# Moving the operands of the large products to multiples of 512 bytes in SBUF

## The chip, the cores and the metric

The kernel runs on one core of one Trainium2 chip. The metric is the device time of one execution in microseconds (us). A core has a matrix engine (TensorE; PE in the profile, and PEld for its loads of stationary operands), a vector engine (VectorE, DVE), an activation engine (ScalarE, ACT), GpSimd (POOL) and a queue engine (SyncE, SP) that here only issues transfers. Working memory (SBUF) has 128 partitions; a tile lies at the same byte offset in every partition. Products are summed in PSUM.

A matrix product of the engine has a stationary operand, which is loaded first (128 rows of 128 columns here), and a moving operand, which streams through it column by column. Both are read from SBUF.

## The reference

One inference step of a four-layer network over 128 context tokens and 512 latent tokens of width 1024, in float32. Each layer has a token mixer and an MLP, each with modulation and a layer norm:

```
for l in range(4):                            # mixers: linear attention, conformer, short conv, linear attention
    h = x * (1 + scale) + shift               # modulation from the conditioning vectors
    x = layer_norm(alpha * x + gate * mixer(h))
    h = x * (1 + scale2) + shift2
    x = layer_norm(alpha * x + gate2 * (square(relu(h @ w1)) @ w2))    # w1 [1024, 4096], w2 [4096, 1024]
```

The mixers are themselves mostly products with weights [1024, 1024] to [1024, 3072]. Outputs are both token streams and the final states of the linear attention.

## The kernel before, in words

All 640 tokens are handled together, in five tiles of 128 tokens. Each large product is made of three products in a single-pass float32 format (float32r): weights and activations are split into a high and a low part, and high x high, high x low and low x high are summed in PSUM. The tiles in which these operands lie are:

- `hT` (L459): the sublayer's input, features on partitions, [128, 2 parts, 8 k tiles, 640 tokens]. `put_hT` (L394 to L399) and, for the first sublayer, `opening` (L530, L531) fill it.
- `whi`, `wlo` (L105, L106): the two parts of a weight tile [128, 1024], six buffers each. `split` makes them from the staged float32 tile `st` (L112, five buffers): ScalarE rounds (L107), VectorE subtracts (L108).
- `act` (L1160): the squared ReLU of the MLP, eight tiles [128, 2 parts, 640 tokens]; `a` (L1095): the same for the short convolution.

There are two kinds of large product. `mm1_steps` (L138 to L148) gives output with features on partitions: the weight part is stationary and `hT` moves, 384 tokens in one group and 256 in the next; a group is 8 k tiles x 3 = 24 matmuls. `mm2_steps` (L181 to L195) gives output with tokens on partitions: an activation tile (`hT`, `act` or `a`) is stationary and 512 columns of the weight part move; again 24 matmuls a group. Only the very last token tile of the kernel is done in two groups of 256 columns (`finish`, L916). Two smaller products in the same format form the gates of the linear attention (L685): the stationary operand is `low` or `za`, the moving one lies in the same `low` tile or in `wgb`. TensorE's order is written out by hand: a virtual clock (`beat`, L93) counts columns / 2400 us per matmul and puts work that waits for others between products.

SBUF tiles are placed by pools, one behind the other in the order in which pools and tiles are first asked for: `const` (`cm`, `ones`, `mhalf`, `hT`, `x0` to `x4`, `ident`, `prm`, `tri`, `mask`), then `stage` (`st`), `wp` (`whi`, `wlo`) and the others, and at the end a pool for the current sublayer. A tile's start is rounded up to 32 bytes. So a tile's size sets where everything behind it starts. `mhalf` (the constant -0.5, 8 columns), `ident` (a 128 x 128 identity), `cu0` and `cu1` (inputs of the short convolution) and `acc` (running sums of a modulation in the MLP) are such tiles. The starts, as the built program has them, in bytes within a partition:

| tile | start before | over a multiple of 512 |
|---|---|---|
| hT | 17696 | 288 |
| st | 84000 and each 4096 on | 32 |
| whi, wlo | 104480 to 149536, each 4096 on | 32 |
| za, wgb (gate products, heads 2 and 3) | 161824, 165920 | 32, 32 |
| low (gate products, heads 0 and 1) | 183360 and 198720 | 64 |
| a | 184384 and each 5120 on | 64 |
| act | 187392 and each 5120 on | 0 |

Within these tiles the slices that a matmul reads are whole multiples of 512 bytes apart (128 columns of 4 bytes, or 2560 or 20480 bytes), so the last column holds for each operand of the large products. The exception is the gates' first factor, whose weight tile has slices of 96 columns.

Of the kernel before, what the change touches and what calls it, by code (L numbers as in the profile page):

```python
# [38 lines left out]
class Filler:  # L39
    """Products for the tensor engine to run while a chain of dependent steps waits for other engines."""  # L40

# [25 lines left out]
class Net:  # L67
# [19 lines left out]

# [1 line left out]
    def after(self, us, fn):  # L89
# [12 lines left out]

# [1 line left out]
    def split(self, src, n=1024):  # L104
# [14 lines left out]
    @contextmanager  # L119
    def behind(self, t):  # L120
        """Keeps the vector engine's work in it behind the parts of token tile t's next input."""
        with ExitStack() as held:
            for half in range(2 if (t, 0) in self.marks else 0):
                held.enter_context(self.tc.issue_after(self.marks[t, half]))
            yield
# [10 lines left out]

# [1 line left out]
    def mm1_steps(self, ps, w, c0, n, m=128):  # L138
        """Yields the microseconds of each instruction, as the other generators of products do."""
        i = 0  # L140
        for kt in range(KT):
            for a, h in ((0, 0), (0, 1), (1, 0)):
                self.nc.tensor.matmul(  # L143
                    ps[:m, :n], w[a][:, kt * m:(kt + 1) * m], self.hT[:, h, kt, c0:c0 + n],
                    start=(i == 0), stop=(i == 3 * KT - 1),
                )
                i += 1
                yield self.beat(n / 2400)  # L148
# [24 lines left out]

# [1 line left out]
    def mm2(self, srcs, lhs, epi):  # L175
# [31 lines left out]

# [1 line left out]
    def mod_queue(self, l):  # L209
        """Queues layer l's modulation by groups of 2048 columns: a k tile at a time on the tensor engine, or,  # L210
        where the groups fall in an MLP, two k tiles of 512 columns at a time on the vector engine."""
        self.mods[l] = {"T": self.modp.tile([128, 48, 2], F32, tag="modT", name="modT", bufs=3)}
        for g in range(1 if l == self.layers[0] else 0, 3):
            if (l, g) in MOD_DVE:
                for v in (2 * g, 2 * g + 1):
                    for half in range(2):
                        for p in range(4):
                            self.fill.append((l, g, partial(self.mod_dve, l, v, half, p)))
            else:
                for kt in range(KT):  # L220
                    self.fill.append((l, g, partial(self.mod_step, l, g, kt)))
# [21 lines left out]
    def tail(self, us, fn):  # L243
        """Runs fn once: us later, or before the next part of a modulation."""
        def once():
            if self.mod_tail is once:
                self.mod_tail = None
                fn()

        self.mod_tail = once  # L250
        self.after(us, once)

    def mod_bank(self, l, cols):
        """A bank for the sums, and the bias of each quarter of its rows."""
        ps = self.ps.tile([128, 512], F32, tag="md", name="md", bufs=1)
        mrow = self.row.tile([128, 512], F32, tag="mrow", name="mrow")
        n = 128 // len(cols)
        for t, c in enumerate(cols):
            self.nc.gpsimd.dma_start(
                mrow[n * t:n * t + n, :], self.d["mod_b"][l:l + 1, c:c + 512].broadcast_to([n, 512]))  # L260
        return ps, mrow
# [39 lines left out]
    def mod_dve(self, l, v, half, p):  # L301
        """Vector v's half: two k tiles more of the products, added up per partition; the tensor engine sums those."""
        nc, m = self.nc, self.mods[l]
# [44 lines left out]
    def affine(self, l, sub, prev):  # L348
        """A, B with modulate(LN(x)) = xhat * A + B per feature; prev = (l, i) of the LN."""
        nc = self.nc  # L350
# [23 lines left out]

# [1 line left out]
    def stats(self, a, b, eps):  # L376
        """mean, (var + eps) ** -0.5 and -mean * that over two [128, 512] halves."""
        nc = self.nc
# [15 lines left out]
    def put_hT(self, hf, k0, t):  # L394
        """hf [128, n, 128]: features of k tiles k0.. of token tile t, split into hT."""
        dst = lambda h: self.hT[:, h, k0:k0 + hf.shape[1], t * 128:(t + 1) * 128]
        self.nc.scalar.copy(dst(0), hf)
        self.mark = self.nc.vector.tensor_tensor(out=dst(1), in0=hf, in1=dst(0).bitcast(F32), op=AL.subtract)  # L398
        self.marks[t, k0 > 0] = self.mark.ins  # L399
# [47 lines left out]

# [1 line left out]
    def start(self):  # L449
# [6 lines left out]
        nc.vector.memset(self.ones, 1.0)  # L456
        self.mhalf = const.tile([128, 8], F32, name="mhalf")
        nc.vector.memset(self.mhalf, -0.5)
        self.hT = const.tile([128, 2, KT, NTOK], F32R, name="hT")  # L459
        self.x = [const.tile([128, D], F32, name=f"x{t}") for t in range(TT)]  # L460
        self.mod_queue(self.layers[0])
        self.constant("ident", [128, 128])
        self.units = []
# [13 lines left out]
    def opening(self, products, raw, tmp):  # L477
        """The first sublayer's input, k tile by k tile as its shift and scale come in: unit u of the first
        layer's modulation holds those of features 128 u.. for all inputs. products(u): what tile u is for."""
        nc = self.nc  # L480
# [57 lines left out]

# [1 line left out]
    def gla(self, l, j, nxt):  # L540
        nc, d, tc = self.nc, self.d, self.tc
        with ExitStack() as ctx:
# [8 lines left out]
            def gate_w(dst, hd):  # L551
                """Two heads of the gates' second factor, against z_hi, z_lo, z_hi and 1, 1: w_hi, w_hi, w_lo, b_hi, b_lo."""
                st = self.stage.tile([128, 1024], F32, tag="st", name="st")
# [112 lines left out]
            def chunks(a, par):  # L666
                """[128, 640] -> the chunks of one parity: [128, 5, 64]."""
                return a.rearrange("p (c b k) -> p c b k", b=2, k=64)[:, :, par]
# [4 lines left out]
            def core1(hd):  # L673
# [34 lines left out]
                for i in range(2):  # L708
# [3 lines left out]
                    self.mark = nc.vector.tensor_tensor(out=Em[i], in0=q[hd, 1], in1=Em[i], op=AL.mult)  # L712
                # per tile: the keys of the chunk that comes first, decayed to its end, and both chunks' decay
                F1 = q[hd, 0].rearrange("p (d c k) -> p d c k", d=2, k=64)
# [171 lines left out]
    def out_proj(self, w, lhs, nxt, last):  # L886
        """The sublayer's last product with the residual, and the layer norm token tile by token tile."""
        self.mm2(w[0], lhs, self.residual(0))
# [11 lines left out]
    def finish(self, w, lhs):  # L900
        """The last token tile, its second half of columns in two parts to have less to do after the last product."""
        nc, t = self.nc, TT - 1
# [31 lines left out]

# [1 line left out]
    def conformer(self, l, j, nxt):  # L936
        nc, d, tc = self.nc, self.d, self.tc
        with ExitStack() as ctx:
# [50 lines left out]
            def convolve(c, scr, meanwhile=None):  # L989
                """Four taps of 32 channels a pass: partition (s, channel) holds the row shifted by s."""  # L990
                f = 5 * ROW
# [21 lines left out]
            def add_bias():  # L1013
                """x += b_pw2 * gate, for the second product's bias."""
                self.flush()
# [68 lines left out]

# [1 line left out]
    def shortconv(self, l, j, nxt):  # L1086
        nc, d, tc = self.nc, self.d, self.tc
        with ExitStack() as ctx:
            sb = ctx.enter_context(tc.tile_pool(name="sc", bufs=1))
            cus = []  # L1090
            for i in range(2):
                cu = sb.tile([128, 770], F32, name=f"cu{i}")
                nc.gpsimd.memset(cu, 0.0)
# [48 lines left out]

# [1 line left out]
    def mlp(self, l, ln_next, last):  # L1144
        nc, d, tc = self.nc, self.d, self.tc
        with ExitStack() as ctx:
            sb = ctx.enter_context(tc.tile_pool(name="mlp", bufs=1))
            self.acc = sb.tile([128, 2, 512], F32, name="acc")
            self.load_gate(l, "g2")
# [37 lines left out]
    def more_banks(self, more):  # L1187
        """Three banks more for products, except where linear attention has them."""
        if not more:
# [23 lines left out]
def _layout(inp):  # L1213
# [26 lines left out]
    def stat(w, order=None):  # L1240
        """[1024, M] -> output tiles [M/128, 128, 8 * 128]."""
        t = w.reshape(KT, 128, -1, 128).transpose(2, 1, 0, 3)
        return (t if order is None else t[order]).reshape(-1, 128, KT * 128)

    def mov(w):
        """[1024, 512 n] -> [n, 4, 128, 2 * 512]."""
        return w.reshape(4, 2, 128, -1, 512).transpose(3, 0, 2, 1, 4).reshape(-1, 4, 128, 1024)
# [51 lines left out]
```

## Time and profile before

| | before |
|---|---|
| device time, median of 3 runs (lowest, highest) | 3054.25 us (3054.06, 3059.77) |
| span of the profiled execution, first to last instruction | 3051.8 us |
| what lies around the span in the median run | 2.45 us |
| mean granted TensorE clock, share of 2.4 GHz | 0.996 |
| busy share: PE, PEld, DVE, ACT, POOL | 98%, 86%, 61%, 33%, 5% |
| mean DMA rate | 115 GB/s |

The profiled execution has no time of its own beside its span; the median of the three runs stands for it. Matmuls are pipelined, and the duration given for one includes its way through the engine, so durations overlap: what one costs in a stream is the distance from its start to the next one's. The chain of waits shows this directly, since a piece of it with a count (x24) is the time from the first start to the start of whatever follows.

### The profile page before, as it was taken

The page shows a single profiled execution, that of the slowest core. Times are in us where ns is not written, and L with a number is a line of the kernel's source. Part 1 is how long each engine was busy: PE and PEld are TensorE (multiplying, and loading weights), DVE is VectorE, ACT ScalarE, POOL GpSimd, SP SyncE. Part 2 cuts the span into 40 slices and gives each one's busy share as a digit, 9 for nine tenths or more (in the row PEclk, how much of TensorE's full clock was granted, in tenths as well). Part 3 has the DMA queues.
Part 4 walks back from the last instruction along what each step waited for, and adds up shares of the span by engine and source line. Part 5 has one row for each costly group of instructions (what it writes and reads, how often), then busy time and mean ns, then how long its engine had stood idle before and what let it go on. Part 6 is the DMA issues. An engine that isn't in the chain of part 4 may idle for free.

```text
span 3051.8 us, 42170 instructions
## 1 busy us (share of the span) xinstructions
PE 3003.6 (98%) x17452; PEld 2619.4 (86%) x17452; DVE 1850.7 (61%) x2737; ACT 998.5 (33%) x1592; POOL 153.6 (5%) x295
## 2 busy tenths in 40 slices
PE   7999999999999899999999999999999999999998
PEld 5887798898898697888999988988988887998997
DVE  4445877767597775775384485773465448644345
ACT  4333433232242351332242152321344434322221
POOL 0000100000010010000010010000010001000000
PEclk9999999999999999999999999999999999999999
DMA  6334244445164425453232133552213312222120
GB/s 245 120 121 162 87 132 155 152 144 171 62 182 127 129 97 163 148 174 97 72 111 77 63 118 107 170 162 66 82 69 120 104 64 89 101 90 74 58 90 35
DMA packets 101792, 350.28 MB, mean 115 GB/s; under 512 B 12940, under 2 KB 18572, under 8 KB 101600
## 3 DMA queue, kind: packets, MB, share of 16 engines
q1 hardware_dynamic: 91888, 317.79, 31.6%
q0 software_dynamic: 9712, 29.80, 3.0%
q8 instruction: 137, 2.24, 0.3%
q14 instruction: 55, 0.45, 0.0%
HBM read 340.29 MB, written 7.24 MB: 114 GB/s over the span
## 4 chain that ended last, share of the span: by engine, by line
PE 95%; DVE 2%; DMA 1%; ACT 1%; issue 1%; POOL 0%; SPq 0%; DVEq 0%; POOLq 0%; ACTq 0%
PE mx L143 23%; PE mm L189 22%; PE mx L189 21%; PE mm L143 18%; PE md L273 1%; PE mx L1003 1%; PE md L338 1%; PE tp L408 1%; PE tp L777 1%; PE o L797 1%; PE o L763 1%; PE tp L747 1%; PE tp L724 1%; PE mm L1003 0%; ACT whi L107 0%
## 5 line engine op out<-in xcount | busy, mean ns | idle before, releaser
L107 ACT CAST whi<-st 128x1024 fp32r<-128x1024 f32 (+1 forms) x378 | 395.7, 1050 | 1118.1 <-PE mx L189 301.4
L143 PE MATMUL mx<-hT,whi 128*128 128x256 f32 (+1 forms) x3216 | 706.8, 310 | 1.6 <-DVE hT L398 1.3
L108 DVE TENSOR_TENSOR wlo<-st,whi 128x1024 fp32r<-128x1024 f32 (+1 forms) x378 | 460.0, 1221 | 377.7 <-ACT whi L107 375.9
L143 PE MATMUL mm<-hT,whi 128*128 128x384 f32 (+1 forms) x2592 | 566.6, 309 | 1.2 <-DVE hT L398 0.7
L143 PEld LDWEIGHTS mx<-hT,whi 128*128 128x128 f32 x3216 | 541.9, 189 | 6.0 <-DVE hT L398 2.8
L143 PE MATMUL mx<-hT,wlo 128*128 128x384 f32 (+1 forms) x1608 | 497.8, 310 | 0.0
L189 PE MATMUL mx<-whi,act 128*128 128x512 f32 (+1 forms) x1536 | 493.6, 395 | 0.0
L143 PEld LDWEIGHTS mm<-hT,whi 128*128 128x128 f32 x2592 | 434.1, 189 | 5.4 <-DVE hT L398 1.6
L143 PE MATMUL mm<-hT,wlo 128*128 128x256 f32 (+1 forms) x1296 | 399.7, 308 | 0.0
L189 PEld LDWEIGHTS mx<-whi,act 128*128 128x128 f32 x1536 | 287.4, 187 | 70.8 <-issue 1.7
L189 PE MATMUL mm<-whi,act 128*128 128x512 f32 (+1 forms) x1040 | 336.2, 394 | 0.0
L143 PEld LDWEIGHTS mx<-hT,wlo 128*128 128x128 f32 x1608 | 304.4, 189 | 2.5 <-issue 2.5
L189 PE MATMUL mx<-wlo,act 128*128 128x512 f32 (+1 forms) x768 | 303.4, 395 | 0.0
L320 DVE SCALAR_TENSOR_TENSOR acc<-st,cm,acc 128x512 f32<-128x512 f32 x392 | 275.8, 745 | 36.0 <-ACT acc L318 34.6
L189 PE MATMUL mm<-whi,hT 128*128 128x512 f32 x888 | 286.1, 395 | 0.0
L143 PEld LDWEIGHTS mm<-hT,wlo 128*128 128x128 f32 x1296 | 245.3, 189 | 7.2 <-issue 6.7
L189 PEld LDWEIGHTS mm<-whi,act 128*128 128x128 f32 x1040 | 194.5, 187 | 47.8 <-issue 1.7
L189 PE MATMUL mm<-wlo,act 128*128 128x512 f32 (+1 forms) x520 | 205.1, 394 | 0.0
L189 PEld LDWEIGHTS mm<-whi,hT 128*128 128x128 f32 x888 | 165.5, 188 | 31.9
L204 DVE TENSOR_TENSOR mx<-mx,gate 128x512 f32<-128x512 f32 x120 | 83.5, 696 | 172.7 <-PE mx L189 172.6
L189 PEld LDWEIGHTS mx<-wlo,act 128*128 128x128 f32 x768 | 144.0, 187 | 41.0 <-issue 7.5
L189 PE MATMUL mm<-wlo,hT 128*128 128x512 f32 x444 | 177.3, 399 | 0.0
(250 smaller groups left out, 3157.8 us busy)
## 6 DMA issues: line engine op xcount, KB each, us to landing
st<-in_w SPq DMA_DIRECT2D x256, 512.0 KB, 3.6
st<-in_modv SPq DMA_DIRECT2D x112, 512.0 KB, 4.1
st<-in_modw SPq DMA_DIRECT2D x80, 512.0 KB, 4.7
st<-in_gvr SPq DMA_DIRECT2D x32, 512.0 KB, 5.5
st<-in_cpw SPq DMA_DIRECT2D x24, 512.0 KB, 4.9
st<-in_scin SPq DMA_DIRECT2D x24, 512.0 KB, 3.5
ur<-uscr SPq DMA_DIRECT2D x40, 238.0 KB, 5.9
st<-in_gqk SPq DMA_DIRECT2D x16, 512.0 KB, 5.1
```

Source lines behind the costliest of these rows:

```text
L107: self.nc.scalar.copy(hi[:, :n], src)
L108: self.nc.vector.tensor_tensor(out=lo[:, :n], in0=src, in1=hi[:, :n].bitcast(F32), op=AL.subtract)
L143: self.nc.tensor.matmul(ps[:m, :n], w[a][:, kt * m:(kt + 1) * m], self.hT[:, h, kt, c0:c0 + n], start=(i == 0), stop=(i == 3 * KT - 1),)
L189: self.nc.tensor.matmul(ps, lhs(kt, h, t), s[a][:, c + cols.start:c + cols.stop], start=(i == 0), stop=(i == 3 * nk - 1))
L204: self.nc.vector.tensor_tensor(out=ps, in0=ps, in1=g, op=AL.mult)
L273: nc.tensor.matmul(ps[32 * t:32 * t + 32, :], self.cm[:, kt, :], st[t // 2][:, c:c + 512], start=(kt == 0), stop=(kt == KT - 1),)
L320: nc.vector.scalar_tensor_tensor(out=acc[:, s], in0=w, scalar=c, in1=acc[:, s], op0=AL.mult, op1=AL.add)
L338: nc.tensor.matmul(ps[r:r + 32, :], self.ones, acc[:, s], start=True, stop=True)
L408: nc.tensor.transpose(tp[:, i * 128:(i + 1) * 128], x[:, k * 128:(k + 1) * 128], self.ident)
L724: nc.tensor.matmul(sp[:, i, dd], self.tri[:, 2 + dd], G[:, t0 + i, dd], start=True, stop=True)
L747: nc.tensor.matmul(sc[:, i], Em[i][:, ts], Ep[i][:, ts], start=True, stop=True)
L763: nc.tensor.matmul(o[t], P[t % 2][:, 2], v[t], start=(t % 2 == 0), stop=False)
```

## The change

Four tiles get a few unused columns, so that what lies behind them starts at a multiple of 512 bytes. Nothing that is computed changes, and on each of the five engines the same instructions stand in the same order as before; only the fill of `mhalf` and of `cu0` gets wider by the unused columns (two instructions). The diff also blanks comments, which is left out here; from L463 on, line numbers are higher by one.

```diff
@@ start
-        self.mhalf = const.tile([128, 8], F32, name="mhalf")
+        self.mhalf = const.tile([128, 64], F32, name="mhalf")
         nc.vector.memset(self.mhalf, -0.5)
         self.hT = const.tile([128, 2, KT, NTOK], F32R, name="hT")
...
-        self.constant("ident", [128, 128])
+        self.ident = const.tile([128, 192], F32, name="ident")[:, :128]
+        nc.sync.dma_start(self.ident, d["ident"])
@@ shortconv
-                cu = sb.tile([128, 770], F32, name=f"cu{i}")
+                cu = sb.tile([128, 770 + 120 * (1 - i)], F32, name=f"cu{i}")
@@ mlp
-            self.acc = sb.tile([128, 2, 512], F32, name="acc")
+            self.acc = sb.tile([128, 1032], F32, name="acc")[:, :1024].rearrange("p (s c) -> p s c", s=2)
```

The starts in the changed program:

| tile | start after | over a multiple of 512 |
|---|---|---|
| hT | 17920 | 0 |
| st | 84480 and each 4096 on | 0 |
| whi, wlo | 104960 to 150016, each 4096 on | 0 |
| za, wgb | 162304, 166400 | 0, 0 |
| low | 183840 and 199200 | 32 |
| a | 185344 and each 5120 on | 0 |
| act | 187904 and each 5120 on | 0 |

Tiles that are not operands of the large products shift too: `x0` to `x4` from 288 to 0 over a multiple of 512, the conformer's `u`, `y` and `ur` and the MLP's `acc` from 0 to 480, the linear attention's `q`, `k`, `E` and `G` from 64 to 32. The program's last byte in SBUF moves from 228352 to 228864.

## Rows read from the trace of the kernel before

**Rows 1.** The page, part 1: busy time, share of the span, instructions.
```profile
PE 3003.6 (98%) x17452; PEld 2619.4 (86%) x17452; DVE 1850.7 (61%) x2737; ACT 998.5 (33%) x1592; POOL 153.6 (5%) x295
```

**Rows 2.** Granted clock of the core: span, share of full speed.
```profile
core 0: 3051.8 us, clock 0.996
```

**Rows 3.** Matmuls of L143: count, ns min/median/max, first and last start, forms.
```profile
L143 PE MATMUL mx<-hT,whi x3216: 278/334/446, 378.9 to 2985.5; 128*128 128x384 f32 x99, 128*128 128x256 f32 x91
...
L143 PE MATMUL pa<-hT,wlo x24: 333/334/346, 2258.0 to 2271.8; 128*128 128x384 f32 x16, 128*96 128x384 f32 x8
```

**Rows 4.** Matmuls of L189, stationary act, hT and a.
```profile
L189 PE MATMUL mx<-whi,act x1536: 280/394/502, 443.5 to 3038.9; 128*128 128x512 f32 x190, 128*128 128x256 f32 x2
...
L189 PE MATMUL mm<-whi,hT x888: 387/389/586, 62.7 to 2590.2; 128*128 128x512 f32 x178
...
L189 PE MATMUL mm<-wlo,act x520: 278/396/503, 438.2 to 3041.6; 128*128 128x512 f32 x171, 128*128 128x256 f32 x3
...
L189 PE MATMUL mx<-wlo,hT x116: 387/389/476, 340.9 to 2583.6; 128*128 128x512 f32 x116
L189 PE MATMUL mx<-whi,a x96: 389/396/473, 1733.1 to 1791.4; 128*128 128x512 f32 x96
...
L189 PE MATMUL mm<-wlo,a x32: 395/396/396, 1738.9 to 1784.7; 128*128 128x512 f32 x32
```

**Rows 5.** Chain of waits, MLP of layer 3: start us, us, work and count.
```profile
2625.16 2.87 PE mm L143 x24
2628.03 4.16 PE mx L143 x24
...
2649.13 5.60 PE mm L189 x24
```

**Rows 6.** Chain of waits in the conformer's second product (stationary hT).
```profile
1030.51 2.54 PE mx L189 x11
...
1034.10 3.00 PE mx L189 x13
...
1050.48 5.44 PE mm L189 x24
```

**Rows 7.** Timeline of PE, the last tile's 256-column groups: start us, us, work.
```profile
3036.30 0.28 PE L189 MATMUL mx<-wlo,act 128*128 128x256 f32 x1
...
3041.72 0.28 PE L189 MATMUL mm<-whi,act 128*128 128x256 f32 x1
```

**Rows 8.** Gate products, L685: count, ns min/median/max, first and last start, forms.
```profile
L685 PE MATMUL tp<-low x20: 277/282/384, 60.6 to 2351.6; 98*128 98x256 f32 x20
...
L685 PE MATMUL tp<-wgb,za x20: 283/283/283, 197.0 to 2480.9; 98*128 98x256 f32 x20
```

**Rows 9.** Timeline of PE around four gate products with low (64 over).
```profile
129.20 0.63 PE L685 MATMUL tp<-low 98*128 98x256 f32 x4
129.67 0.39 PE L189 MATMUL mm<-whi,hT 128*128 128x512 f32 x1
```

**Rows 10.** The same with za and wgb (32 over).
```profile
196.98 0.64 PE L685 MATMUL tp<-wgb,za 98*128 98x256 f32 x4
197.46 0.40 PE L189 MATMUL mm<-whi,hT 128*128 128x512 f32 x1
```

**Rows 11.** DVE, one 128x640 subtraction into act (0 over) and a (64).
```profile
L1163 DVE TENSOR_TENSOR act<-r,act x128: 809/825/828, 406.5 to 2989.7; 128x640 fp32r<-128x640 f32 x128
L1125 DVE TENSOR_TENSOR a<-y,a x8: 816/819/819, 1597.3 to 1735.4; 128x640 fp32r<-128x640 f32 x8
```

**Rows 12.** Waits of PE for transfers: us in total, times, longest.
```profile
PE md L487 <- DMA st<-in_modw: 11.7, 5, 7.2
PE mm L1003 <- DMA ur<-uscr: 3.8, 1, 3.8
```

## Prediction, made before the changed kernel was run

> **What bounds the kernel now.** I read part 1 of the page first: PE is busy for 98% of the span, 3003.6 of 3051.8 us [rows 1]. The reader is to see that no other engine comes near. The clock comes next, since it would scale everything: the granted share is 0.996, so TensorE runs at the higher of its two levels, 2.4 GHz, throughout [rows 2]. What is left to read is what one matmul costs in the stream, and there the chain of waits is the best view: a piece with a count of 24 is one group of a large product from its first start to the next start. A group of 256 columns takes 2.87 us, one of 384 takes 4.16, one of 512 with `act` stationary 5.60 [rows 5], one of 512 with `hT` stationary 5.44 [rows 6]. By 24 that is 119.6, 173.3, 233.3 and 226.7 ns a matmul. At 2.4 GHz the columns alone need 106.7, 160.0 and 213.3 ns. So there is a surplus of 13 ns at 256 and 384 columns and with `hT` stationary, and of 20 ns with `act`. In units of 16 columns, 6.67 ns and 64 bytes of a moving operand, that is two units or three.
>
> The counts: L143 has 8784 matmuls in six rows, of which the first and the last stand in [rows 3]; half of them are 384 wide and half 256, 4392 each. L189 has four rows with `act` (1536 to 520, in all 3864, of which 48 are 256 wide), four with `hT` (888 to 116, in all 1680), four with `a` (96 to 32, in all 240) [rows 4]. The surplus of all is 4392 x 12.9 + 4392 x 13.3 + 1680 x 13.4 + 4056 x 20 = 219 us. That is the most that placement could ever give back, and the change touches nothing else of weight.
>
> **What the trace says of placement.** The weight tiles that move are the same in the two kinds of 512-column group; only the stationary tile differs, `hT` at 288 bytes over a multiple of 512 or `act` at 0. The medians of the durations are 389 against 394 to 396 ns, and `a`, at 64 over, stands with `act` at 396 [rows 4]. 288 is 32 over a multiple of 64; 0 and 64 are multiples of 64. In L143 the stationary tile is a weight part, at 32 over, and its surplus is that of `hT`: two units. So a stationary tile that starts 32 bytes into a 64-byte unit goes with a steady surplus of two units, and one on a multiple of 64 with a larger one at 512 columns.
>
> What such a tile does at 256 columns is shown in two places. In the last token tile `act` is stationary and 256 columns move: from 3036.30 to 3041.72 us there are 46 steps, 117.8 ns each [rows 7], which is less than the 119.6 of L143. And the gate products: with `za` and `wgb`, both at 32 over, each of them takes the same 283 ns, while with `low`, both operands at 64 over, they scatter from 277 to 282 (the 384 is one that stands apart) [rows 8]. Four of them run from start to next start in 0.48 us in the first case, 120 ns each [rows 10], and in 0.47 in the second, 117.5 each [rows 9]. With `low` the moving operand too is on a multiple of 64, and it gains nothing over the last token tile, where it is 32 off. So the rule that fits all the rows looks only at the stationary operand: 32 over, two units at any width; a multiple of 64, some 11 ns at 256 columns and 20 at 512.
>
> **The change part by part.** No instruction moves on any engine. What changes is the offsets: weights 32 to 0, `hT` 288 to 0, `a` 64 to 0; `act` stays at 0.
>
> - L143, 256 columns: the stationary weights come onto a multiple of 64. 119.6 becomes 117.8: 4392 x -1.8 = -7.9 us. The other end is no change, 0.
> - L143, 384 columns: no row has this width with a stationary tile on a multiple of 64. Halfway between 117.8 and 233.3 lies 175.6, against 173.3 now: 4392 x +2.3 = +10.1 us, the value I take. Ends: 171.1 (117.8 plus 128 columns at full speed, 53.3), -9.7 us; and 180.0 (the full 20 ns of the 512 columns), +29.4 us.
> - L189 with `hT`: 226.7 becomes 233.3, 1680 x 6.6 = +11.1 us at most. Not all of them run at 226.7: the pieces of 11 and 13 after an interruption take 2.54 and 3.00 us, some 231 each [rows 6]. I take two thirds, +7.4 us; the other end is 0.
> - L189 with `act` and `a`: stationary on a multiple of 64 before and after, 0.
> - Everything that is no large product: VectorE takes 825 ns for a subtraction into a tile at 0 and 819 for the same one at 64 [rows 11], so shifting its tiles is worth under 1% there, and PE's 98% cover it. Wider fills of `mhalf` and `cu0` lie off the path. Transfers land in `st` at 0 instead of 32 and in `ur` at 480 instead of 0; PE waits for these two for 11.7 and 3.8 us in the whole run [rows 12]. I cost them at nothing; a tenth of those waits, either way, would be 1.6 us.
>
> Sum: -7.9 + 10.1 + 7.4 = +9.6 us, with ends of -17.6 (-7.9 - 9.7 + 0) and +40.5 (0 + 29.4 + 11.1). The span becomes 3051.8 + 9.6 = 3061.4; with the 2.45 us between span and median, 3063.9 us, and the ends 3037 and 3095. The measurement tells 0.2% from no change, some 6 us, so this forecast is only just slower.
>
> **The rivals.**
>
> Nothing happens. It may be the place of the tile and not its alignment: `act`, `a` and `low` all lie above byte 183000, `hT`, the weights and `za` below 167000, and no stationary operand of these products tells the two readings apart. Then the time stays at 3054. For the alignment speaks that a step of 32 bytes in 64 is a natural one and the border between 167000 and 183000 isn't.
>
> The Trainium skill speaks for this rival: "SBUF — State Buffer", section "Specifications (TRN2)", gives lines of 16 bytes, and 0, 32, 64 and 288 are all multiples of 16. "TensorE: Matmul & The Clock Gate", section "Step-by-step: what each phase is for", gives the moving and the stationary operand a read port each, by which the stationary tile's place couldn't slow a stream. By both the time would be as before. The trace disagrees with the second: the same moving tiles take 226.7 or 233.3 ns with the one or the other stationary tile.
>
> It is the offset between the two operands that counts. `hT` and weights are 256 bytes apart (0 in units of 64), and so are `za` and `wgb` (0): two units. `act` and `a` are 32 off the weights: three. After the change all are 0 apart and all would pay two units: 4056 x 6.67 = 27 us less, 3027 us, faster. Against it: `low` has both operands at the same offset and doesn't show the steady 120 [rows 8, 9].
>
> The moving operand's start counts, but only at more than 64 bytes. No large product's moving operand is on a multiple of 512 now. If its alignment takes one unit from every product, that is (4392 x 2 + 1680 + 4056) x 6.67 = 97 us, 2957 us. For it: surpluses come in just such units. Against it: `low`, the only case with an aligned moving operand, won 2.5 ns at most.
>
> [...]
>
> The operands collide. If both streams begin at the same place in a multiple of 512 and every product then pays the three units that `act` pays now, at any width, that is 4392 x 7.1 + 4392 x 6.7 + 1680 x 6.6 = 72 us more, 3126 us, much slower. It decides once the groups of 256 pass 126 ns. Against it: `za` and `wgb` are at the same offset now and pay two units.
>
> **How the numbers follow.** The forecast (the stationary tile's rule) gets 0.44: between its ends it is over 6 us slower with about 0.26, within 6 us with 0.14, faster with 0.04. Nothing happens: 0.13. The offset between operands: 0.16. The moving operand: 0.16. Collision: 0.11. Faster is 0.04 + 0.16 + 0.16 = 0.36; same 0.14 + 0.13 = 0.27; slower 0.26 + 0.11 = 0.37. The likeliest case alone has the range 3037 to 3095. Down from there I go to the offset between operands (3027) and to the one unit less (2957), so the range is 2950 to 3095. Outside lie most of the collision and a part of the moving operand's case that goes further, together under 0.2.
>
> **What would show it.** In the chain after, groups of 256 at 2.83 us, of 384 at about 4.21, of 512 at 5.60 with any stationary tile: the rule holds. Groups of 512 at 5.44 with `act`: the offset between operands. 2.71, 4.00 and 5.28 or 5.44: the moving operand counts. Unchanged pieces: the place. 3.04, 4.32 and 5.60: collision. The forecast is wrong above all if groups of 384 go below 4.16.

## The result

The changed kernel takes 3028.71 us (median of 4 runs, 3025.92 to 3032.24), the kernel before in the same comparison 3056.91 (4 runs, 3054.06 to 3059.77): ratio 0.9909, 95% interval 0.9895 to 0.9923. In a second comparison, on the chip of the split kernel below, the ratio was 0.9928 (0.9915 to 0.9942). The forecast of 3064, slightly slower, was wrong; the time is that of the rival in which the offset between the two operands counts (3027).

The page's part 1 of the changed kernel (busy time, share, instructions), against [rows 1]:

```profile
PE 2978.6 (98%) x17452; PEld 2620.9 (87%) x17452; DVE 1850.4 (61%) x2737; ACT 999.6 (33%) x1592; POOL 154.5 (5%) x295
```

PE's busy time falls by 25.0 us, the span by 23.8, from 3051.8 to 3028.0; the other engines change by 1.5 us at most. The clock's share is 0.995 after 0.996. Where the 25 us come from is shown by the matmuls of L189 and L143 (ns min/median/max), against [rows 3, 4]:

```profile
L189 PE MATMUL mx<-whi,act x1536: 277/389/499, 443.9 to 3015.1; 128*128 128x512 f32 x190, 128*128 128x256 f32 x2
...
L189 PE MATMUL mm<-whi,hT x888: 387/389/586, 62.3 to 2572.5; 128*128 128x512 f32 x178
...
L189 PE MATMUL mm<-wlo,act x520: 283/389/499, 438.7 to 3017.9; 128*128 128x512 f32 x171, 128*128 128x256 f32 x3
```

```profile
L143 PE MATMUL mx<-hT,whi x3216: 278/334/446, 379.5 to 2963.1; 128*128 128x384 f32 x99, 128*128 128x256 f32 x91
```

The products with `act` stationary go from 394 and 396 ns to 389, the figure that `hT` had and keeps. The row of L143 stays as it was to the nanosecond. The chain of waits says the same in groups of 24 (start us, us, work); in the MLP of layer 3, against [rows 5]:

```profile
2610.31 4.16 PE mx L143 x24
2614.48 2.87 PE mm L143 x24
...
2647.76 5.44 PE mm L189 x24
```

and for `hT` in the conformer, against [rows 6], and below it for `a`, in the short convolution:

```profile
1046.47 5.44 PE mm L189 x24
...
1729.04 5.44 PE mm L189 x24
```

Only the groups with `act` and `a` changed, 5.60 to 5.44 us, 6.67 ns a matmul: (3816 + 240) x 6.67 = 27.0 us if all of them run in this rhythm. Two small groups matter for the argument. The 256-column groups of the last token tile got dearer: from 3012.49 to 3018.01 us 46 steps, 120.0 ns each, where [rows 7] had 117.8 (timeline of PE):

```profile
3012.49 0.28 PE L189 MATMUL mx<-wlo,act 128*128 128x256 f32 x1
...
3018.01 0.28 PE L189 MATMUL mm<-whi,act 128*128 128x256 f32 x1
```

And the gate products with `low`, now at 32 over instead of 64, kept their times, against [rows 8]:

```profile
L686 PE MATMUL tp<-low x20: 277/282/384, 60.3 to 2335.0; 98*128 98x256 f32 x20
...
L686 PE MATMUL tp<-wgb,za x20: 282/283/283, 197.5 to 2463.2; 98*128 98x256 f32 x20
```

### The profile page after: what moved, and what is told of

It reads as the page before. It is cut to its first block, busy times and chain, and to the rows that moved or that the text cites. A ratio compares the mean times of both kernels' runs of the same rounds, so it can differ in the third digit from the quotient of the medians.

```text
span 3028.0 us, 42170 instructions
## 1 busy us (share of the span) xinstructions
PE 2978.6 (98%) x17452; PEld 2620.9 (87%) x17452; DVE 1850.4 (61%) x2737; ACT 999.6 (33%) x1592; POOL 154.5 (5%) x295
## 4 chain that ended last, share of the span: by engine, by line
PE 95%; DMA 2%; DVE 1%; ACT 1%; issue 1%; POOL 0%; SPq 0%; DVEq 0%; ACTq 0%; POOLq 0%
PE mx L143 23%; PE mm L189 22%; PE mx L189 20%; PE mm L143 19%; PE md L273 1%; PE md L338 1%; PE mx L1004 1%; PE tp L408 1%; PE o L798 1%; PE tp L778 1%; PE tp L725 1%; PE o L764 1%; DMA st<-in_gvr 1%; PE tp L748 1%; PE mm L1004 1%
## 5 line engine op out<-in xcount | busy, mean ns | idle before, releaser
L143 PE MATMUL mx<-hT,whi 128*128 128x256 f32 (+1 forms) x3216 | 706.9, 310 | 1.7 <-DVE hT L398 1.5
L143 PE MATMUL mm<-hT,whi 128*128 128x384 f32 (+1 forms) x2592 | 566.4, 309 | 1.1 <-DVE hT L398 0.8
L143 PEld LDWEIGHTS mx<-hT,whi 128*128 128x128 f32 x3216 | 541.9, 189 | 5.9 <-DVE hT L398 3.0
L143 PE MATMUL mx<-hT,wlo 128*128 128x384 f32 (+1 forms) x1608 | 497.8, 310 | 0.0
L189 PE MATMUL mx<-whi,act 128*128 128x512 f32 (+1 forms) x1536 | 484.7, 389 | 0.0
L143 PEld LDWEIGHTS mm<-hT,whi 128*128 128x128 f32 x2592 | 434.0, 189 | 5.0 <-DVE hT L398 1.7
L143 PE MATMUL mm<-hT,wlo 128*128 128x256 f32 (+1 forms) x1296 | 399.7, 308 | 0.4 <-DVE wlo L108 0.4
L189 PEld LDWEIGHTS mx<-whi,act 128*128 128x128 f32 x1536 | 287.9, 188 | 61.1 <-issue 1.7
L189 PE MATMUL mm<-whi,act 128*128 128x512 f32 (+1 forms) x1040 | 330.2, 388 | 0.0
L143 PEld LDWEIGHTS mx<-hT,wlo 128*128 128x128 f32 x1608 | 304.4, 189 | 2.5 <-issue 2.5
L189 PE MATMUL mx<-wlo,act 128*128 128x512 f32 (+1 forms) x768 | 299.2, 390 | 0.0
L189 PE MATMUL mm<-whi,hT 128*128 128x512 f32 x888 | 286.1, 395 | 0.0
L143 PEld LDWEIGHTS mm<-hT,wlo 128*128 128x128 f32 x1296 | 245.2, 189 | 7.8 <-issue 6.7
L189 PEld LDWEIGHTS mm<-whi,act 128*128 128x128 f32 x1040 | 194.8, 188 | 41.2 <-issue 1.7
L189 PE MATMUL mm<-wlo,act 128*128 128x512 f32 (+1 forms) x520 | 202.3, 389 | 0.0
L189 PEld LDWEIGHTS mm<-whi,hT 128*128 128x128 f32 x888 | 165.5, 188 | 31.9
L189 PE MATMUL mm<-wlo,hT 128*128 128x512 f32 x444 | 177.3, 399 | 0.0
L189 PEld LDWEIGHTS mx<-wlo,act 128*128 128x128 f32 x768 | 144.3, 188 | 36.3 <-issue 7.5
```

The costliest lines, as they stand in the source:

```text
L143: self.nc.tensor.matmul(ps[:m, :n], w[a][:, kt * m:(kt + 1) * m], self.hT[:, h, kt, c0:c0 + n], start=(i == 0), stop=(i == 3 * KT - 1),)
L189: self.nc.tensor.matmul(ps, lhs(kt, h, t), s[a][:, c + cols.start:c + cols.stop], start=(i == 0), stop=(i == 3 * nk - 1))
```

## The experiments

Below, "distance" is the start of the stationary operand minus that of the moving one, in bytes within a partition. In L189 the stationary operand is `act`, `a` or `hT` and the weights move; in L143 it is the other way round.

**One tile alone.** The kernel before, with `act` put at the weights' remainder. Of the other tiles only `r` moves, by the same 32 bytes: it lies between `acc` and `act` and is no operand of a product.

```diff
-            self.acc = sb.tile([128, 2, 512], F32, name="acc")
+            self.acc = sb.tile([128, 1032], F32, name="acc")[:, :1024].rearrange("p (s c) -> p s c", s=2)
```

> The kernel before with one edit: acc gets 8 unused columns, so act starts at 32 over a multiple of 512, like the weight tiles (32); hT stays at 288, a at 64, the weights at 32, and no large product's operand lies on a multiple of 512. Theory A (what counts is the distance between stationary and moving operand in units of 64 bytes; a remainder of 32 costs a third unit at 512 columns): groups of 24 with act stationary go from 5.60 to 5.44 us, 3816 x 6.67 = 25 us, all but some interrupted ones, so 3031 us, ratio 0.992. Theory B (operands must lie on multiples of 64 or 512 themselves): nothing is gained, act even leaves its multiple, 3054 to 3057 us. Theory C (the gain came from other tiles that shifted: st, x, the conformer's tiles): 3054 to 3057 us. The forecast's rule (a stationary tile at 32 over goes with two units) also says 3031 here, but it had said 5.60 for the changed kernel.

Measured: 3031.65 us, ratio 0.9926 (0.9912 to 0.9939). Matmuls with `act` and with `a`:

```profile
L189 PE MATMUL mx<-whi,act x1536: 277/389/499, 446.9 to 3020.3; 128*128 128x512 f32 x190, 128*128 128x256 f32 x2
...
L189 PE MATMUL mx<-whi,a x96: 389/396/480, 1724.0 to 1782.4; 128*128 128x512 f32 x96
```

Moving `act` by 32 bytes, off its multiple of 512, gives what the whole change gives, within the intervals. `a`, whose distance is still 32, stays at 396. That rules out theory B and theory C: neither multiples of 512 nor the shift of `st`, `x` or the conformer's tiles is needed.

**The distance put back.** The changed kernel, with `act` and `a` 32 bytes on:

```diff
-                cu = sb.tile([128, 770 + 120 * (1 - i)], F32, name=f"cu{i}")
+                cu = sb.tile([128, 770 + 128 * (1 - i)], F32, name=f"cu{i}")
...
-            self.acc = sb.tile([128, 1032], F32, name="acc")[:, :1024].rearrange("p (s c) -> p s c", s=2)
+            self.acc = sb.tile([128, 1040], F32, name="acc")[:, :1024].rearrange("p (s c) -> p s c", s=2)
```

> The changed kernel with act and a moved 32 bytes on (acc 1040 columns, cu0 898): hT and the weights at multiples of 512, act and a at 32 over. Theory A: the distance is 32 again, groups of 24 with act or a at 5.60 us, the whole gain is lost, 3054 to 3057 us, ratio 1.000. Theory B: hT and the weights keep their alignment, so the larger part of any gain stays; with only the stationary operand off, below 3045 us. Theory C: all other tiles lie as in the changed kernel, so 3029 us. The forecast's rule (stationary 32 over: two units): 3029 us.

Measured: 3056.45 us, ratio 1.0009 (1.0000 to 1.0018). In the chain, `hT` and then `act`:

```profile
1045.69 5.44 PE mm L189 x24
...
2663.18 5.60 PE mm L189 x24
```

The gain is gone. Here `act` lies 32 over, where the forecast's rule promised 5.44, and pays 5.60. With the first experiment this leaves the distance. Written as (stationary, moving), each in bytes over a multiple of 512, (0, 32) and (32, 0) are dear, (0, 0) and (32, 32) cheap.

**hT off by 32.** The changed kernel, with `hT` 32 bytes on:

```diff
-        self.mhalf = const.tile([128, 64], F32, name="mhalf")
+        self.mhalf = const.tile([128, 72], F32, name="mhalf")
...
-        self.ident = const.tile([128, 192], F32, name="ident")[:, :128]
+        self.ident = const.tile([128, 184], F32, name="ident")[:, :128]
```

> The changed kernel with hT (and x) moved 32 bytes on (mhalf 72 columns, ident 184); act, a and the weights stay at multiples of 512. Theory A: all products with hT get a distance of 32: L143 behaves as the last token tile did, groups of 256 at 2.83 us instead of 2.87, groups of 384 between 4.11 and 4.32 (halfway 4.21), groups of 512 with hT at 5.60 instead of 5.44; with act 5.44 as in the changed kernel. In all 4392 x -1.8 + 4392 x 2.3 + 1680 x 6.6 x 2/3 = +10 us (ends -18 and +41) over the changed kernel: 3039 us. The forecast's rule (only the stationary tile counts): L143 unchanged with its weights at 0, and L189 with hT at 32 unchanged too: 3029 us.

Measured: 3035.05 us, ratio 0.9937 (0.9924 to 0.9951), span 3029.6 us. Chain of waits: `hT` stationary, then L143 at 256 and 384 columns, then `act`, then L143 again, later in the same MLP:

```profile
1045.92 5.60 PE mm L189 x24
...
2608.72 2.80 PE mm L143 x24
2611.52 4.16 PE mx L143 x24
...
2648.74 5.44 PE mm L189 x24
...
2736.25 4.24 PE mx L143 x24
2740.49 2.83 PE mm L143 x24
```

The products with `hT` change and those with `act` don't, as the distance demands. But at this one distance L143 runs in two rhythms, which last for stretches of several groups: 2.80 or 2.83 us at 256 columns, 4.16 or 4.24 at 384. Of the groups of 384 that run uninterrupted in the trace, 71 take 4.16 and 81 take 4.24, and the mean of all 161 is 4.21, the figure expected. What chooses the rhythm is open. The total is less clear: the ratio lies above that of the changed kernel in its first comparison (0.9909) and can't be told apart from that in its second (0.9928).

**The unit.** Three runs, one execution each, gave `act` another distance in each layer: the pad of `acc` depends on the layer. The first had 32, 64, 96 and 128 bytes, and moved the gates' moving part in the `low` tile 512 bytes further from the stationary one:

```diff
-            self.acc = sb.tile([128, 1032], F32, name="acc")[:, :1024].rearrange("p (s c) -> p s c", s=2)
+            self.acc = sb.tile([128, 1032 + 8 * (l + 1)], F32, name="acc")[:, :1024].rearrange("p (s c) -> p s c", s=2)
...
-                low.update(z=new[0:98, 0:NTOK], w=new[0:98, NTOK:NTOK + 512])
+                low.update(z=new[0:98, 0:NTOK], w=new[0:98, NTOK + 128:NTOK + 640])
```

> The changed kernel with act moved on by 32 bytes in layer 0, 64 in layer 1, 96 in layer 2 and 128 in layer 3; and the gate products' moving part in the low tile lies 512 bytes further from the stationary one (3072 instead of 2560 bytes). Theory A with units of 64 bytes: groups of 24 with act at 5.60, 5.44, 5.60, 5.44 us in layers 0 to 3. With units of 128 bytes: 5.60, another value, 5.60, 5.44. With multiples of 512: none at 5.44. For the low tile: if its scatter (277 to 282 ns) hangs on the distance of 2560 bytes, it turns into the steady 283 of za and wgb; otherwise it stays.

The chain of waits, a group in each of layers 0 to 3:

```profile
456.62 5.60 PE mm L189 x24
...
1308.25 5.60 PE mm L189 x24
...
2086.68 5.62 PE mm L189 x24
...
2665.00 5.57 PE mm L189 x24
```

Units of 64 bytes are refuted: a distance of 64 pays as much as one of 32. The `low` tile's scatter stayed (277, 282, 384). The second run had 160, 192, 224 and 256, and, by pads that are left out here, 256 for `a` and 128 for `hT`:

```diff
-            self.acc = sb.tile([128, 1032], F32, name="acc")[:, :1024].rearrange("p (s c) -> p s c", s=2)
+            self.acc = sb.tile([128, 1032 + (40, 48, 56, 64)[l]], F32, name="acc")[:, :1024].rearrange("p (s c) -> p s c", s=2)
```

> The changed kernel with act moved on by 160, 192, 224 and 256 bytes in layers 0 to 3, a by 256, hT (and x) by 128; the weights stay at multiples of 512. The scan before showed 5.60 us a group of 24 at distances 32 and 64, 5.62 at 96 and 5.57 at 128, so the unit isn't 64 bytes. Theory A2 (the distance counts in units of 256 bytes; in the kernel before hT and the weights were 256 apart and ran at 5.44): layers 0 to 2 at 5.57 to 5.62, layer 3 and a at 5.44. If the unit is 512, layer 3 and a are near 5.6 too, and the 5.44 of hT before had another reason. hT at 128: groups of 512 with hT at 5.57 as act at 128; L143 like in the run with hT 32 off (2.83 at 256, about 4.19 at 384).

Layers 0 to 3, with `hT` stationary between layer 0 and layer 1, with `a` between layer 1 and layer 2, and L143 before layer 3:

```profile
459.32 5.60 PE mm L189 x24
...
1056.06 5.57 PE mm L189 x24
...
1312.56 5.49 PE mm L189 x24
...
1743.26 5.44 PE mm L189 x24
...
2090.91 5.60 PE mm L189 x24
...
2640.45 2.85 PE mm L143 x24
...
2650.38 4.22 PE mm L143 x24
...
2673.80 5.44 PE mm L189 x24
```

At 256 the cheap rhythm is back, to the digit, for `act` and for `a`. `hT` at 128 costs what `act` cost there, 5.57. The third run went beyond, to 288, 320, 384 and 480, with 128 for `a` and 64 for `hT`; the pad of `acc` is the same with (72, 80, 96, 120).

> The changed kernel with act moved on by 288, 320, 384 and 480 bytes in layers 0 to 3, a by 128, hT (and x) by 64. Theory A2 (units of 256 bytes): layer 0 like a distance of 32 (5.60 us a group of 24), layer 1 like 64 (5.60), layer 2 and a like 128 (5.57), layer 3 like 224. Unit of 512: other values at 288 to 480 than at 32 to 224. hT at 64: groups of 512 with hT at 5.60. No distance is expected below 5.44; one that is would show that the two units of surplus aren't fixed.

Layers 0 to 3, and L143 with `hT` 64 on:

```profile
459.25 5.60 PE mm L189 x24
...
1309.93 5.60 PE mm L189 x24
...
2102.85 5.57 PE mm L189 x24
...
2609.38 2.83 PE mm L143 x24
...
2627.67 4.16 PE mx L143 x24
...
2665.43 5.60 PE mm L189 x24
```

The values repeat: 288 is as 32, 320 as 64, 384 as 128, 480 as 224. So for these products the distance counts in units of 256 bytes. Theory A2 holds, with one exception that it didn't foresee: 192 costs 5.49, only 0.05 more than a distance of 0. It was measured in one layer of one run.

**A faster version.** Groups of 256 columns are cheaper with the moving operand 32 bytes on, those of 384 and 512 are not. So `hT` was put in two tiles, tokens 0 to 383 (`CA` is 384) at a multiple of 512 and the other 256 (`CB`) at 32 over. In `opening` each part is then written by itself, which is left out here, as is the pad that is taken off `ident`:

```diff
-        self.hT = const.tile([128, 2, KT, NTOK], F32R, name="hT")
+        self.hA = const.tile([128, 2, KT, CA], F32R, name="hT")
+        self.hB = const.tile([128, 8 + 2 * KT * CB], F32R, name="hTb")[:, 8:].rearrange("p (h k t) -> p h k t", h=2, k=KT)
...
+    def hs(self, h, kt, c0, n):
+        a, c = (self.hA, c0) if c0 < CA else (self.hB, c0 - CA)
+        return a[:, h, kt, c:c + n]
```

> The changed kernel with hT in two tiles: tokens 0 to 383 at a multiple of 512, tokens 384 to 639 at 32 over; the opening writes each part by itself (32 instructions instead of 16). The run with hT 32 off showed 256-column matmuls 2.2 ns cheaper and 384-column ones 1.2 dearer on average; here only the 256 wide ones get the distance. Theory A2: 4392 x -2.2 = -9.7 us in L143, and two of five token tiles with hT stationary pay 4.6 ns more, 1680 x 2/5 x 4.6 = +3.1; together -6.6 us against the changed kernel, some 3022 us, ratio to the kernel before 0.989, if the opening doesn't get longer by its 16 added instructions (at most 8 x some 0.3 us).

> The changed kernel once more, on the same chip as the split one, to compare the two: ratio to the kernel before 0.991 as in its first comparison.

Measured: the split kernel 3021.79 us, ratio 0.9895 (0.9882 to 0.9909); the changed kernel on the same chip 3031.33, ratio 0.9928 (0.9915 to 0.9942). The intervals don't touch: splitting wins some 9.5 us over the change, where 6.6 were expected. Chain of waits: the second part of `hT` stationary, its first part, then L143 at 384 and 256:

```profile
1050.05 5.60 PE mx L189 x24
1055.65 5.44 PE mm L189 x24
...
2604.12 4.16 PE mx L143 x24
2608.29 2.80 PE mm L143 x24
```

183 groups of 256 (4392 / 24) win up to 0.07 us each, 12.8 us at most; nearly all that run uninterrupted take 2.80 here, not 2.83. The 672 products of L189 with the second part pay up to 6.67 ns each, 4.5 us at most. By these two 8.3 us would be left; PE's busy time is 10.2 us lower than in the changed kernel on this chip, 2969.3 after 2979.5.

**The witness that misled.** The changed kernel, with the gates' moving part of layer 0 in another tile, far from the stationary one and again a multiple of 256 from it (the two added lines make L686 L688):

```diff
+                if l == self.layers[0]:
+                    low["w"] = self.bc.tile([128, 1024], F32R, tag="ag", name="wlow")[0:98, 8:520]
```

> The changed kernel with one edit: in layer 0, heads 0 and 1, the gate products' moving part lies not in the low tile behind the stationary part but some 21000 bytes below it (from byte 162336), again a multiple of 256 from it. So far these products scatter (277 to 282 ns) at distances of 2560 and 3072 bytes, both multiples of 256, where za and wgb, and all large products, run steadily (283). If it is that both operands lie in one stretch of SBUF, the products of layer 0 turn to 283 and those of layer 3 stay; if it is the stationary tile's place alone or something in what runs before, layer 0 keeps 277 to 282.

Measured, in one execution of 3030.72 us:

```profile
L688 PE MATMUL tp<-wgb,za x20: 282/283/283, 195.9 to 2464.2; 98*128 98x256 f32 x20
...
L688 PE MATMUL tp<-wlow,low x10: 278/282/385, 59.2 to 132.2; 98*128 98x256 f32 x10
L688 PE MATMUL tp<-low x10: 277/282/283, 2264.1 to 2335.7; 98*128 98x256 f32 x10
```

The scatter stays. It hangs neither on the remainder of 64 or 32, nor on 2560 or 3072 bytes between the operands, nor on one stretch of SBUF for both. What makes `low` scatter is open; the stationary tile's place and the products around it are left. For the second speaks the run with `hT` 32 bytes on:

```profile
L686 PE MATMUL tp<-wgb,za x20: 278/283/288, 197.3 to 2463.6; 98*128 98x256 f32 x20
```

`za` and `wgb` lie there as in the changed kernel, where the same 20 products took 282 to 283 ns, and yet they scatter. What moved is `hT`, an operand of the products just before and just behind, and with it `x`. So a burst of four shows its neighbours too, and not its own operands alone.

## Why the prediction was wrong

- What bounds the kernel was right: PE, and in it the step from one matmul's start to the next. The span followed PE's busy time, 23.8 of 25.0 us. The surplus in units of 16 columns held for the change, where `act` lost one unit, but it is no rule: at distances of 192 and 128 groups take 5.49 and 5.57 us, a surplus of 15.4 and 18.8 ns, neither two units nor three.
- The step that failed is "the rule that fits all the rows looks only at the stationary operand". The runs put in its place the distance between the operands, in units of 256 bytes. In the kernel before, a stationary tile at 32 over a multiple of 64 always had a moving one 0 or 256 bytes off, and one on a multiple of 64 had a moving one 32 off. So the two rules agreed on every large product. The prediction had the other rule among its rivals, and gave it 0.16 against 0.44.
- What decided between them was `low`: 0.47 against 0.48 us, four products in a burst, and a scatter of 277 to 282 ns. Its operands have a distance that is a multiple of 256 and yet it doesn't run steadily. The argument against the right rival rested on that alone, and the experiments show that it tells nothing of remainders: `za` and `wgb` lose their steadiness when only a neighbour's operand moves.
- The three terms that followed from the rule (-7.9, +10.1 and +7.4 us in L143 and with `hT`) came to nothing: the rows of these products are unchanged, since they had a good distance before and kept it. The term that was set to 0, `act` and `a`, is the whole effect.
- The last token tile was read rightly as another rhythm, 117.8 against 119.6 ns, and it became 120.0 with a distance of 0. Cheaper at 256 columns and dearer at 512 go with one and the same distance, as the run with `hT` 32 off shows. The price at 384 taken halfway, 4.21 us, is met there only as a mean of 4.16 and 4.24, and the change itself brought no product to that state.
- The right rival's size was nearly right: 27 us, against 28.2 between the medians, 21.8 in the second comparison and 25.0 in PE's busy time. Its unit wasn't, and it was luck that this made no difference: the changed kernel brings the large products' distances to 0, which is a multiple of any unit, and before it only 0, 32 and 256 bytes occurred. That the time lies in the range of 2950 to 3095 is no merit of the rule either: the rivals stretched it down, the rule's own ends are 3037 and 3095. The collision (72 us slower) and the moving operand's own alignment (97 us faster) didn't happen.
- One reading was too strong: the clock isn't at its higher level throughout. From 1003.70 to 1007.10 us of the kernel before, the granted clock was 0.51 of 2.4 GHz, near the lower level of 1.2 GHz, after PE had been busy for 0.07 of 3.70 us. The sum doesn't suffer, since the means of the two kernels are 0.996 and 0.995.
- Costing the rest at nothing was right: PE's wait for `st` in the opening is 11.5 us after 11.7, for `ur` 3.7 after 3.8.

The Trainium skill's read ports ("TensorE: Matmul & The Clock Gate", section "Step-by-step: what each phase is for") would let neither operand's place matter, and its lines of 16 bytes ("SBUF — State Buffer", section "Specifications (TRN2)") would make all these starts alike. The traces disagree with both as far as they were applied here: 5.44 or 5.60 us a group with `act` stationary, by the distance of 0 or 32 bytes alone.

## What to carry to other kernels

Where a stream of single-pass float32 products bounds a kernel, work out the distance of the two operands' starts modulo 256 bytes for each kind of product, and read the price of each from the steps of the chain, by width: of the distances tried here, 0 was best at 512 columns, and at 256 the one with the moving operand 32 bytes on. One pad of 32 bytes in front of the right tile did, within the intervals, what a change of four tiles did. When two rules fit all the strong rows, look for the row in which they differ by much, and count a burst of four products as no such row: it carries the rhythm of what runs around it.

## What was not expected of the hardware

For products in this format, 128 stationary columns and a clock share of 0.995, a group of 24 at 512 columns took, by the distance modulo 256: 0, 5.44 us; 32 and 64, 5.60; 96, 5.62; 128, 5.57; 160, 5.60; 192, 5.49; 224, 5.60. It is not symmetric: 64 short of a multiple (192) is nearly free, 64 beyond it isn't. The narrower groups of L143 have prices of their own. With `hT` 32 bytes on, a distance of -32, they take 2.80 or 2.83 us at 256 columns and 4.16 or 4.24 at 384; with 64, 2.83 and 4.16; with 128, 2.85 and 4.22; at 0 it is 2.87 and 4.16. So the distance doesn't fix the rhythm wholly, and what else does is open. That loads of the stationary operand and the moving stream get in each other's way in SBUF, and fall in step or out of it, would fit much of this, but it is only argued; no run here shows the reads themselves. Even at the best distance some 13 ns a matmul remain over the columns' time at 512 and 384 columns.
